# Two decoder layers on one core: the order around the second norms, and the place of a branch hint

## The chip, the core and the metric

One NeuronCore of a Trainium2 chip runs the whole program in one launch. TensorE (PE in the profile, its weight loads PEld) multiplies matrices, VectorE (DVE), ScalarE (ACT) and GpSimd (POOL) work on tiles of 128 partitions in SBUF, sums of products land in PSUM banks, and SyncE (SP) issues most of the DMA transfers between HBM and SBUF. The metric is the device time of one launch in microseconds (us).

## What is computed

Two layers of a decoder, 512 tokens of width 1024 in float32. Layer 0 mixes tokens with two groups of recurrent heads, layer 1 with sparse attention over chosen keys. Behind each mixer stand a norm, a mixture of 16 experts (each token goes to two of them) and a second norm:

```
x = LN(alpha*x + mixer(x))                 # first norm, ln1g, ln1b
x = LN(alpha*x + MoE(x))                   # second norm, ln2g, ln2b

def _layer_norm(x, g, b):
    mu, var = mean(x), mean((x - mu)**2)
    return (x - mu) * rsqrt(var + eps) * g + b

def _moe(h, ...):                          # s = sigmoid(h @ router_w), 4 groups of 4 experts
    best group, its top two experts, gate = s / sum of the two s
    for e in range(16):
        he = (silu(h @ w_gate[e]) * (h @ w_up[e])) @ w_down[e]
        y = y + comb[:, e:e+1] * he
```

## The kernel before

Tokens lie in four tiles of 128 (NT), features in eight chunks of 128 (KC). Every float32 product is made of three: a weight tile `wr` arrives by DMA, ScalarE casts it to a rounded high part `wh` (L581), the difference to it is the low part `wl` (L582, on VectorE, or on GpSimd where a letter of a string says `p`), and TensorE adds high x high, low x high and high x low (L68 to L70). `LO1 = "pvvp"` holds these letters for the four groups of layer 1's mixer weights: the first is `w1a` (972, 972 and 648 columns in three loads), the second `w1b`.

The gate (`route`, from L800) ranks the tokens of each expert with the matmuls `cum`, keeps TensorE going with the `busy` ones (L817), and makes for each expert the list of its 128 token slots with the matmuls `lst` (`lists(0, 2)`, then `lists(2, 5)`). If an expert has more than 128 tokens, `rovf` is 1 and extra blocks run. Each engine loads `rovf` into a register and branches on it (L1093 and L1094); in the runs shown the blocks are jumped over, a few hundred rows of TensorE's program. `k.soon(engine, ins)` places a branch prefetch hint for that branch on the engine behind the instruction `ins`.

The experts then run in order: gather of rows `xg` by GpSimd, transposition `xt`, products `gu`, `htp`, `yo`, and scatter of the result `ys` into Y in HBM by GpSimd's indirect DMA (L1088) with addition. The last two experts are not scattered: their `yo` is split in `wh`, `wl` and added by TensorE.

The second norm reads Y back into the tiles Z (`hy<-Y`, L1126), and for each token tile TensorE sums Z and the last experts' rows in two PSUM banks `zt` (L1136, ten matmuls a tile). `BANKS` names the banks of the tiles. VectorE's order is written out in `TAIL`, a token for each step and tile: `s` statistics (L613 to L623; ScalarE takes the square root, L621), `r` root (reciprocal and one Newton step in L631 and L632, then times -1/2 in L1151), `c` centring with the gain (L1147), `f` finish (times the root, plus b; L1155), `n` root and ScalarE's norm out of PSUM (L1167, L1169), `g`, `h`, `p` gain and bias (L1172, L1173) on VectorE and GpSimd, on VectorE alone, on GpSimd alone, `d` the tile's next use, `e` finish and store by halves (L1160). In layer 0 `d` stands for the tile's transposition `x1tp` (L1203), its split `th`, `tl`, and then layer 1's first products `pq` with `w1a`; in layer 1 for the store of the output.

```
stt(Z[i][:, cs], zp_, S[i][0][:, 0:1], g[:, cs], op0=ALU.subtract, op1=ALU.mult)   # c: L1147
stt(Z[i], Z[i], S[i][1], b, op0=ALU.mult, op1=ALU.add)                             # f: L1155
```

On SyncE the loads of `w1a` stand behind those of Z (`behind(tc, w.loads[n0], k.last_load)`), and `AFTA = "r0"` puts ScalarE's casts of `w1a` behind the square root of tile 0.

Of the kernel before, what the change touches and what calls it, by code (L numbers as in the profile page):

```python
# [15 lines left out]
ALU = mybir.AluOpType  # L16
# [19 lines left out]
ROPE, LO1 = 512, "pvvp"  # L36
PAD = 2
BANKS = ("pj pj sv sv pj pj sv sv", "pj pj sv sv sm sm sm ch")
AFTA, AFTB = "r0", "x2 y2"

TAIL = ["s0 c0 r0 f0 s1 n1 s2 n2 d0 g1 s3 g2 c3 d1 r3 f3 d2 d3", "s0 n0 s1 n1 p1 h0 s2 d0 c2 d1 s3 r2 c3 f2 d2 r3 e3"]
# [585 lines left out]
def ln_root(nc, sm, mv, v, y, _=None):  # L627

    nc.vector.reciprocal(y, y)
    a = sm.tile([P, 1], F32, name="lna", tag="lna")  # L630
    nc.vector.scalar_tensor_tensor(a, y, v, y, op0=ALU.mult, op1=ALU.mult)  # L631
    nc.vector.scalar_tensor_tensor(y, a, 3.0, y, op0=ALU.subtract, op1=ALU.mult)  # L632
    return mv[:, 0:1], y


def out_proj_ln(tc, k, L, sm, hp, proj, g, b, order):
# [3 lines left out]
    nc = tc.nc  # L640
# [52 lines left out]
    def rest():  # L693
# [5 lines left out]
        stt(rs[:, 1:2], mu, -1.0, rs[:, 0:1], op0=ALU.mult, op1=ALU.mult)  # L699
# [66 lines left out]
def route(nc, k, rp, sm, hp, lg, rest, dbg=None):  # L766
# [63 lines left out]
    k.soon(mybir.EngineType.PE, k.ranked)  # L830
# [37 lines left out]
    def lists(a, b):  # L868
        for n in range(8):
            m = nc.tensor.matmul(lst[:, a:b].rearrange("p a e -> p (a e)"), E[:, n],  # L870
                             L[:, n, a:b].rearrange("p a e -> p (a e)"), start=n == 0, stop=n == 7)
        return m
# [28 lines left out]
    lists(2, 5)  # L901
# [99 lines left out]
def moe_ln(tc, k, I, L, w, xgp, xgs, tail, dbg):  # L1001
# [3 lines left out]
    with ExitStack() as es:  # L1005
# [63 lines left out]
        def down(e):  # L1069
# [18 lines left out]
            nc.gpsimd.indirect_dma_start(out=k.Y, out_offset=bass.IndirectOffsetOnAxis(ap=tgt[:, e:e + 1], axis=0),  # L1088
# [29 lines left out]
    with ExitStack() as es:  # L1118
# [3 lines left out]
        for v, n in ((g, "ln2g"), (b, "ln2b")):  # L1122
            nc.sync.dma_start(v, I[n][L:L + 1, :].partition_broadcast(P))
        Z = [k.h[:, i] for i in range(NT)]
        for i in range(NT):
            k.last_load = nc.sync.dma_start(Z[i], k.Y[i * P:(i + 1) * P, :])  # L1126
        S, ZP = {}, {}
# [21 lines left out]
        def root(i):  # L1149
            mu, r = ln_root(nc, sm, *S[i])  # L1150
            nc.vector.tensor_scalar(r, r, -0.5, None, op0=ALU.mult)  # L1151
            S[i] = mu, r

        def finish(i):
            stt(Z[i], Z[i], S[i][1], b, op0=ALU.mult, op1=ALU.add)  # L1155

# [20 lines left out]
        step = {"s": stats, "c": centre, "r": root, "f": finish, "e": halves, "n": norm, "g": gain,  # L1177
# [32 lines left out]
def dsa(tc, k, I, es, weights, xt, dbg):  # L1210
# [25 lines left out]
    def chunks(name, grp, ncol, lo=None, late=""):  # L1236
# [6 lines left out]
        behind(tc, w.loads[n0], k.last_load)  # L1243
        k.last_load = w.loads[-1]
# [460 lines left out]
```

## Time and profile before

| | |
|---|---|
| three runs, median (least to most) | 1030.81 us (1030.23 to 1031.31) |
| the profiled execution, its own time | 1034.22 us |
| its span in the trace | 1032.5 us |
| busy: PE, DVE, ACT, POOL | 936.1, 795.6, 563.4, 309.3 us |
| DMA | 174.06 MB, mean 169 GB/s |
| mean granted TensorE clock | 0.974 |

The span is what the trace covers; the execution's own time is 1.7 us longer. A share of busy time is a mean over stages: the mixer of layer 0 up to about 400 us, its gate to 422, its experts to 582, its second norm and layer 1's mixer and gate to 840, layer 1's experts to 1003, its second norm to the end.

### The profile page before, as it was taken

Reading aid. Unit: us, or ns where it says so; the run is one execution under the profiler, and the core shown is the slowest. Engines: PE = TensorE matmul, PEld = TensorE weight load, DVE = VectorE, ACT = ScalarE, POOL = GpSimd, SP = SyncE. Lnnn points to the kernel's source line nnn. Section 1 sums busy time; section 2 is a strip of 40 time slices with the busy share of each in tenths; the row PEclk is TensorE's granted clock in tenths of the full one; section 3 lists DMA queues with packets and bytes.
Section 4 is the critical chain, followed back from the end, with each engine's and each line's share of the span. In section 5 each row is a group of like instructions: output and inputs, shape, how many; then the busy total and the mean of one; then the engine's idle time right before and its main releaser. Section 6 shows DMA issues by size and latency. Waiting matters only on the chain. (4 is left out here: it accounts for less than half of the span.)

```text
span 1032.5 us, 14694 instructions
## 1 busy us (share of the span) xinstructions
PE 936.1 (91%) x4992; PEld 716.2 (69%) x4992; DVE 795.6 (77%) x1690; ACT 563.4 (55%) x911; POOL 309.3 (30%) x235
## 2 busy tenths in 40 slices
PE   7799988997998999899999987998999879999895
PEld 5577756675776878767778667674668767777673
DVE  4637689398398666899999887699964679898886
ACT  6435473334336124588988543436761338888771
POOL 2200202003011003365555323113201335666432
PEclk9899999999899999999999989998999999999998
DMA  6223102212104487899987544102302369999963
GB/s 225 95 67 93 53 8 86 53 52 72 27 1 155 151 276 250 315 362 341 310 303 248 171 127 142 42 1 102 123 21 82 123 242 384 319 322 312 322 234 134
DMA packets 72277, 174.06 MB, mean 169 GB/s; under 512 B 24472, under 2 KB 25784, under 8 KB 72192
## 3 DMA queue, kind: packets, MB, share of 16 engines
q1 hardware_dynamic: 63840, 158.02, 43.6%
q0 software_dynamic: 8352, 15.00, 5.9%
q8 instruction: 42, 0.69, 0.3%
q14 instruction: 43, 0.35, 0.1%
HBM read 162.19 MB, written 26.21 MB: 182 GB/s over the span
## 5 line engine op out<-in xcount | busy, mean ns | idle before, releaser
L581 ACT CAST wh<-wr 128x1024 fp32r<-128x1024 f32 (+2 forms) x233 | 220.5, 955 | 91.9 <-PE pj L69 44.1
L582 DVE TENSOR_TENSOR wl<-wr,wh 128x1024 fp32r<-128x1024 f32 (+1 forms) x193 | 229.7, 1211 | 44.7 <-ACT wh L581 36.1
L582 POOL TENSOR_TENSOR wl<-wr,wh 128x1024 fp32r<-128x1024 f32 (+2 forms) x40 | 103.7, 2597 | 134.0 <-issue 64.6
L69 PE MATMUL gu<-wl,xgh 128*128 128x512 f32 x256 | 103.9, 406 | 8.6 <-PEq L1094 5.3
L68 PE MATMUL gu<-wh,xgh 128*128 128x512 f32 x256 | 102.4, 400 | 3.1 <-DVE xgl L64 2.1
L70 PE MATMUL gu<-wh,xgl 128*128 128x512 f32 x256 | 102.6, 401 | 0.1
L68 PE MATMUL pj<-xh,wh 128*128 128x512 f32 x208 | 87.1, 419 | 9.6 <-ACT xh L63 6.6
L70 PE MATMUL pj<-xh,wl 128*128 128x512 f32 x208 | 86.3, 415 | 0.0
L69 PE MATMUL pj<-xl,wh 128*128 128x512 f32 x208 | 86.2, 415 | 0.0
L1088 POOL DMA_INDIRECT Y<-ys,rtgt x28 | 53.4, 1908 | 80.0 <-ACT ys L1084 18.7
L69 PEld LDWEIGHTS gu<-wl,xgh 128*128 128x128 f32 x256 | 48.9, 191 | 22.7 <-POOL wl L582 6.2
L1014 POOL DMA_INDIRECT xg<-hD,rtgt x30 | 46.6, 1552 | 41.7 <-PEq L1094 11.9
L68 PEld LDWEIGHTS gu<-wh,xgh 128*128 128x128 f32 x256 | 48.8, 191 | 13.7 <-DVE xgl L64 2.2
L70 PEld LDWEIGHTS gu<-wh,xgl 128*128 128x128 f32 x256 | 48.9, 191 | 9.8 <-DVE xgl L64 0.5
L68 PEld LDWEIGHTS pj<-xh,wh 128*128 128x128 f32 x208 | 40.1, 193 | 19.8 <-ACT xh L63 6.6
L69 PE MATMUL yo<-wl,hth 128*128 128x512 f32 x128 | 52.2, 408 | 0.1
L68 PE MATMUL yo<-wh,hth 128*128 128x512 f32 x128 | 50.6, 396 | 1.8 <-ACT hth L63 1.6
L70 PE MATMUL yo<-wh,htl 128*128 128x512 f32 x128 | 50.1, 391 | 0.0
L64 DVE TENSOR_TENSOR xgl<-xtp,xgh 128x512 fp32r<-128x512 f32 x60 | 38.4, 681 | 11.7 <-ACT xgh L63 11.7
L70 PEld LDWEIGHTS pj<-xh,wl 128*128 128x128 f32 x208 | 39.9, 192 | 10.1 <-issue 2.0
L68 PE MATMUL pq<-wh,th 128*128 128x512 f32 (+2 forms) x128 | 46.9, 366 | 0.0
L69 PEld LDWEIGHTS pj<-xl,wh 128*128 128x128 f32 x208 | 40.1, 193 | 9.8 <-issue 1.7
(433 smaller groups left out, 2246.2 us busy)
## 6 DMA issues: line engine op xcount, KB each, us to landing
wr<-in_wgu_dram SPq DMA_DIRECT2D x102, 512.0 KB
wr<-in_wdn_dram SPq DMA_DIRECT2D x50, 512.0 KB
wr<-in_w_dram SPq DMA_DIRECT2D x52, 256.0 KB
wr<-in_wo_dram SPq DMA_DIRECT2D x16, 512.0 KB
hy<-in_wgu_dram SPq DMA_DIRECT2D x15, 512.0 KB
room<-in_wgu_dram SPq DMA_DIRECT2D x11, 512.0 KB
hy<-in_wdn_dram SPq DMA_DIRECT2D x9, 512.0 KB
hD<-hy SPq DMA_DIRECT2D x8, 512.0 KB
```

The source lines that it names most:

```text
L64: nc.vector.tensor_tensor(lo, src, hi.bitcast(F32), op=ALU.subtract))
L68: nc.tensor.matmul(out, ah, bh, start=start, stop=False)
L69: nc.tensor.matmul(out, ah, bl, start=False, stop=False)
L70: return nc.tensor.matmul(out, al, bh, start=False, stop=stop)
L581: nc.scalar.copy(h[:, s], r[:, s])
L582: (lo or nc.vector).tensor_tensor(l[:, s], r[:, s], h[:, s].bitcast(F32), op=ALU.subtract)
L1014: nc.gpsimd.indirect_dma_start(out=xg, out_offset=None, in_=k.hD, in_offset=bass.IndirectOffsetOnAxis(ap=tgt[:, e:e + 1], axis=0), bounds_ ...
L1088: nc.gpsimd.indirect_dma_start(out=k.Y, out_offset=bass.IndirectOffsetOnAxis(ap=tgt[:, e:e + 1], axis=0), in_=ys, in_offset=None, bounds_c ...
```

## The change

It does these things: the three `w1a` loads stand ahead of the Z loads on SyncE, the casts no longer wait for tile 0's root, and their low parts move from GpSimd to VectorE; the Newton step uses two operands per partition as scalars (TENSOR_SCALAR) in place of SCALAR_TENSOR_TENSOR, also in one place of the first norm; the factor -1/2 is multiplied once into the gain vector g by GpSimd, behind its last scatter, and L1151 goes; tile 3 of layer 0 sums in the banks `sm` and `ch`; in layer 1 the root of tile 2 is taken earlier, and its finish becomes a multiplication on ScalarE and an add of b on GpSimd (`k`); TensorE's branch hint moves from behind the `cum` matmuls to behind `lists(2, 5)`.

```diff
-ROPE, LO1 = 512, "pvvp"
+ROPE, LO1 = 512, "vvvp"
...
-BANKS = ("pj pj sv sv pj pj sv sv", "pj pj sv sv sm sm sm ch")
-AFTA, AFTB = "r0", "x2 y2"
+BANKS = ("pj pj sv sv pj pj sm ch", "pj pj sv sv sm sm sm ch")
+AFTA, AFTB = "", "x2 y2"
-TAIL = ["s0 c0 r0 f0 s1 n1 s2 n2 d0 g1 s3 g2 c3 d1 r3 f3 d2 d3", "s0 n0 s1 n1 p1 h0 s2 d0 c2 d1 s3 r2 c3 f2 d2 r3 e3"]
+TAIL = ["s0 c0 r0 f0 s1 n1 s2 n2 d0 g1 s3 g2 c3 d1 r3 f3 d2 d3", "s0 n0 s1 n1 p1 h0 s2 d0 c2 r2 k2 d1 s3 c3 d2 r3 e3"]
...
-    nc.vector.scalar_tensor_tensor(a, y, v, y, op0=ALU.mult, op1=ALU.mult)
-    nc.vector.scalar_tensor_tensor(y, a, 3.0, y, op0=ALU.subtract, op1=ALU.mult)
+    nc.vector.tensor_scalar(a, y, v, y, op0=ALU.mult, op1=ALU.mult)
+    nc.vector.tensor_scalar(y, a, 3.0, y, op0=ALU.subtract, op1=ALU.mult)
...
-        stt(rs[:, 1:2], mu, -1.0, rs[:, 0:1], op0=ALU.mult, op1=ALU.mult)
+        nc.vector.tensor_scalar(rs[:, 1:2], mu, rs[:, 0:1], -1.0, op0=ALU.mult, op1=ALU.mult)
...
-    k.soon(mybir.EngineType.PE, k.ranked)
...
-    lists(2, 5)
+    k.soon(mybir.EngineType.PE, lists(2, 5))
...
-            nc.gpsimd.indirect_dma_start(out=k.Y, out_offset=bass.IndirectOffsetOnAxis(ap=tgt[:, e:e + 1], axis=0),
+            k.sent = nc.gpsimd.indirect_dma_start(out=k.Y, out_offset=bass.IndirectOffsetOnAxis(ap=tgt[:, e:e + 1], axis=0),
...
+        behind(tc, nc.gpsimd.tensor_scalar(g, g, -0.5, None, op0=ALU.mult), k.sent)
         Z = [k.h[:, i] for i in range(NT)]
         for i in range(NT):
             k.last_load = nc.sync.dma_start(Z[i], k.Y[i * P:(i + 1) * P, :])
+            if i == 0:
+                k.first_z = k.last_load
...
         def root(i):
-            mu, r = ln_root(nc, sm, *S[i])
-            nc.vector.tensor_scalar(r, r, -0.5, None, op0=ALU.mult)
-            S[i] = mu, r
+            S[i] = ln_root(nc, sm, *S[i])
...
+        def shift(i):
+            nc.scalar.mul(Z[i], Z[i], S[i][1])
+            nc.gpsimd.tensor_tensor(Z[i], Z[i], b, op=ALU.add)
...
-        behind(tc, w.loads[n0], k.last_load)
-        k.last_load = w.loads[-1]
+        if n0:
+            behind(tc, w.loads[n0], k.last_load)
+            k.last_load = w.loads[-1]
+        else:
+            behind(tc, k.first_z, w.loads[-1])
```

TensorE at the end of layer 0's gate. Before, the hint stands behind the last `cum`, ahead of the `busy`, `xt` and `lst` matmuls:

```order
L827 LDWEIGHTS ones_1371
L827 MATMUL cum<-rM,ones_1371 128x16
L1701 BRANCH_PREFETCH_HINT
L817 MATMUL busy<-c_ident 128x128 x7
L844 MATMUL xt_3817<-xg_3416,hy 128x128 x8
L870 LDWEIGHTS rE
```

At the branch, before:

```order
L870 LDWEIGHTS rE
L870 MATMUL lst<-rL,rE 128x48
L1093 TENSOR_LOAD rovf
L1094 COMPARE_AND_BRANCH
L929 LDWEIGHTS re
```

After, the last `lst` matmuls, the hint, the load of the register and the branch:

```order
L869 LDWEIGHTS rE
L869 MATMUL lst<-rL,rE 128x48
L869 LDWEIGHTS rE
L869 MATMUL lst<-rL,rE 128x48
L1709 BRANCH_PREFETCH_HINT
L1092 TENSOR_LOAD rovf
L1093 COMPARE_AND_BRANCH
L928 LDWEIGHTS re
```

The hint has moved past all of the lists. In layer 1 the same move leaves ten `gu` matmuls and the register load between hint and branch.

TensorE in layer 0's second norm, at the end of the sums of tile 2. Before, the transposition of tile 0 stands ahead of tile 3's ten `zt`:

```order
L1136 MATMUL zt<-wh,onehot 128x512
L1136 MATMUL zt<-wl,onehot 128x512
L1203 MATMUL x1tp<-c_ident,hy 128x128 x8
L1136 MATMUL zt<-hy,c_ident 128x512
L1136 MATMUL zt<-wh,onehot 128x512
```

(Seven more `zt` and then `pq` follow.) After, the last two `zt` of tile 3 stand ahead of the transposition:

```order
L1138 MATMUL zt<-wh,onehot 128x512
L1138 MATMUL zt<-wl,onehot 128x512
L1207 MATMUL x1tp<-c_ident,hy 128x128 x8
L68 MATMUL pq<-wh,th 128x324
L69 MATMUL pq<-wl,th 128x324
```

So 40 `zt` run in one piece, and the first products `pq` follow the transposition of tile 0 directly.

VectorE at the start of the same norm, before (`wl<-yo` are the last expert's low parts):

```order
L64 TENSOR_TENSOR wl<-yo,wh 128x512 x2
L613 BN_STATS bst<-zt 128x6 x2
L619 BN_AGGR bmv<-bst 128x2
L623 TENSOR_SCALAR lnv<-bmv 128x1
L1147 SCALAR_TENSOR_TENSOR hy<-zt,bmv,xg_3417 128x512 x2
L629 RECIPROCAL lny<-lny 128x1
L631 SCALAR_TENSOR_TENSOR lna<-lny,lnv 128x1
L632 SCALAR_TENSOR_TENSOR lny<-lna,lny 128x1
L1151 TENSOR_SCALAR lny<-lny 128x1
L1155 SCALAR_TENSOR_TENSOR hy<-hy,lny,xg_3418 128x1024
```

After, with the low parts of `w1a` (972, 972 and 648 columns):

```order
L582 TENSOR_TENSOR wl<-wr,wh 128x972
L64 TENSOR_TENSOR wl<-yo,wh 128x512 x2
L582 TENSOR_TENSOR wl<-wr,wh 128x972
L613 BN_STATS bst<-zt 128x6 x2
L582 TENSOR_TENSOR wl<-wr,wh 128x648
L619 BN_AGGR bmv<-bst 128x2
L623 TENSOR_SCALAR lnv<-bmv 128x1
L1149 SCALAR_TENSOR_TENSOR hy<-zt,bmv,xg_3417 128x512 x2
L629 RECIPROCAL lny<-lny 128x1
L631 TENSOR_SCALAR lna<-lny,lnv 128x1
L632 TENSOR_SCALAR lny<-lna,lny 128x1
L1155 SCALAR_TENSOR_TENSOR hy<-hy,lny,xg_3418 128x1024
```

Three low parts have come in, the third between the statistics and their aggregate, the two root steps have changed their kind, and the row of L1151 is gone. (Lines of after count from its own file.)

## Rows read from the trace of the kernel before

**Rows 1.** Busy time by stage: layer 0's experts, its second norm with the start of layer 1's mixer, layer 1's experts. Each row: from:to in us, length, busy us of PE, PEld, DVE, ACT, POOL with counts, granted TensorE clock, DMA share, GB/s.

```profile
422.00:582.00 160.00, 154.10 (x726) 123.34 (x727) 148.31 (x163) 132.81 (x183) 84.15 (x43) 0.99 0.86 293
582.00:640.00 58.00, 47.08 (x266) 38.97 (x265) 49.99 (x109) 24.29 (x45) 16.74 (x8) 0.93 0.50 168
840.00:1003.00 163.00, 153.33 (x709) 118.30 (x710) 142.15 (x157) 132.58 (x183) 88.75 (x43) 0.99 0.92 319
```

**Rows 2.** The chain of work that ended last, in order of time: start us, duration us, what.

```profile
842.70 11.68 DMA wr<-in_wdn_dram
...
1006.88 7.39 PE zt L1136 x24
```

**Rows 3.** The loads of `rovf` (L1093) and the branch on it (L1094) as each engine's sequencer ran them in both layers (PEldq is TensorE's, DVEq VectorE's, SPq SyncE's): ns min/median/max, start of the first (layer 0) and of the last.

```profile
L1093 PEldq TENSOR_LOAD <-rovf x2: 310/404/497, 418.4 to 833.0; - x2
...
L1094 SPq EVENT_SEMAPHORE  x18: 17/17/17, 425.2 to 839.6; - x18
L1094 PEldq COMPARE_BRANCH  x2: 393/3399/6405, 419.0 to 833.4; - x2
L1094 SPq COMPARE_BRANCH  x2: 68/69/70, 419.1 to 832.9; - x2
L1094 DVEq COMPARE_BRANCH  x2: 68/70/72, 420.5 to 833.1; - x2
L1094 DVEq EVENT_SEMAPHORE  x2: 21/21/21, 421.1 to 836.2; - x2
```

**Rows 4.** DMA queues by window: first queue 8, of kind instruction, in 409.2 to 419.1 (packets, MB, share); then the lines of 819.2 to 833.4 where queue 8 would stand, between queue 0 and queue 14; then queue 8 in 833.4 to 839.8.

```profile
q8 instruction: 1, 0.02, 0.6%
...
q0 software_dynamic: 144, 0.19, 5.2%
q14 instruction: 3, 0.02, 0.9%
...
q8 instruction: 1, 0.02, 1.1%
```

**Rows 5.** TensorE's timeline at the gates of layer 0 and layer 1: start us, duration, engine, line, operation, count, and in brackets the idle time before it with what ended it.

```profile
409.38 0.24 PE L827 MATMUL cum<-rM,ones 128*128 128x16 bf16 x4
...
421.95 0.51 PE L68 MATMUL gu<-wh,xgh 128*128 128x512 f32 x1 [2.13 <-DVE xgl L64]
...
839.98 0.76 PE L69 MATMUL gu<-wl,xgh 128*128 128x512 f32 x1 [5.35 <-PEq L1094]
```

**Rows 6.** TensorE's waits from 422 to 582: engine, line, who waited <- for whom: us in all, times, longest.

```profile
PE htp L1063 <- DVE hh L1056: 3.3, 10, 1.2
```

**Rows 7.** SyncE's timeline at the start of the second norm of layer 0: DMA issues.

```profile
578.00 1.75 SPq L1126 DMA_DIRECT2D hy<-Y  x4
579.85 1.75 SPq L574 DMA_DIRECT2D wr<-in_w1a_dram  x3
```

**Rows 8.** GpSimd's timeline in the second norm of layer 0; the lines L631 and L632 (ns min/median/max, first and last start); VectorE's timeline in that norm.

```profile
588.71 6.00 POOL L582 TENSOR_TENSOR wl<-wr,wh 128x972 fp32r<-128x972 f32 x3 [15.11 <-DMA wr<-in_w1a_dram]
...
L631 DVE SCALAR_TENSOR_TENSOR lna<-lny,lnv x16: 201/219/2035, 375.3 to 1026.9; 128x1 f32<-128x1 f32 x16
...
L632 DVE SCALAR_TENSOR_TENSOR lny<-lna,lny x16: 140/159/2189, 375.5 to 1027.2; 128x1 f32<-128x1 f32 x16
...
593.25 0.15 DVE L1151 TENSOR_SCALAR lny<-lny 128x1 f32<-128x1 f32 x1
593.44 2.35 DVE L1155 SCALAR_TENSOR_TENSOR hy<-hy,lny,xg 128x1024 f32<-128x1024 f32 x1
...
603.11 1.22 DVE L1172 TENSOR_TENSOR hy<-hy,xg 128x1024 f32<-128x1024 f32 x1
```

**Rows 9.** TensorE's and GpSimd's timelines in the same norm: the first and the last of the first thirty `zt`, the tile transposes `x1tp`, the first product `pq`; then the second add of L1173.

```profile
582.60 1.02 PE L1136 MATMUL zt<-hy,c_ident 128*128 128x512 f32 x2
...
593.12 0.40 PE L1136 MATMUL zt<-wl,onehot 128*128 128x512 f32 x1
595.85 1.09 PE L1203 MATMUL x1tp<-c_ident,hy 128*128 128x128 f32 x8 [2.33 <-DVE hy L1155]
599.57 2.07 PE L1136 MATMUL zt<-hy,c_ident 128*128 128x512 f32 x2 [2.63 <-ACT hy L1169]
...
605.39 0.31 PE L68 MATMUL pq<-wh,th 128*128 128x324 f32 x1
...
607.61 1.03 PE L1203 MATMUL x1tp<-c_ident,hy 128*128 128x128 f32 x8
...
614.09 0.60 PE L1203 MATMUL x1tp<-c_ident,hy 128*128 128x128 f32 x4
...
608.02 2.40 POOL L1173 TENSOR_TENSOR hy<-hy,xg 128x1024 f32<-128x1024 f32 x1 [1.16 <-DVE hy L1172]
```

**Rows 10.** The line L840, which makes 128x128 tables: ns min/median/max, first and last start.

```profile
L840 DVE TENSOR_SCALAR pick<-c_iota,rs x4: 268/1534/2930, 820.3 to 823.4; 128x128 f32<-128x128 f32 x4
```

**Rows 11.** The end of layer 1: GpSimd's and VectorE's timelines.

```profile
1018.27 3.01 POOL L1172 TENSOR_TENSOR hy<-hy,xg 128x1024 f32<-128x1024 f32 x1 [20.93 <-ACT hy L1169]
1021.36 2.34 POOL L1173 TENSOR_TENSOR hy<-hy,xg 128x1024 f32<-128x1024 f32 x1
...
1025.57 1.27 DVE L1155 SCALAR_TENSOR_TENSOR hy<-hy,lny,xg 128x1024 f32<-128x1024 f32 x1
...
1027.58 1.41 DVE L1160 SCALAR_TENSOR_TENSOR hy<-hy,lny,xg 128x512 f32<-128x512 f32 x2
```

More of the change, by code (lines that the diff above doesn't have):

```diff
@@ L1176, in moe_ln @@
             total(i)
-        step = {"s": stats, "c": centre, "r": root, "f": finish, "e": halves, "n": norm, "g": gain,
+        step = {"s": stats, "c": centre, "r": root, "f": finish, "e": halves, "k": shift, "n": norm, "g": gain,
                 "h": lambda i: gain(i, (nc.vector, nc.vector)), "p": lambda i: gain(i, (nc.gpsimd, nc.gpsimd)),
```

## The prediction

> **What bounds the kernel now.** I read the stage table first, because the change sits in four places with different limits [rows 1]. In layer 0's experts (422 to 582 us) TensorE is busy 154.10 of 160 us: what is late there ends the stage later. In layer 1's experts (840 to 1003) the DMA share is 0.92, and the chain that ended last [rows 2] shows why that is the row to look at: from 842.70 on it consists of weight loads, then it goes over the scatters into Y and their reload to the sums `zt` at 1006.88, and behind them to VectorE. Between them, from 582 to 640, TensorE is busy 47.08 of 58: nobody is the bound, and what counts is who waits last.
>
> The run profiled took 1034.22 us for a span of 1032.5 and lies 3.4 us above the median of 1030.81 (runs 1030.23 to 1031.31), more than those three differ. The sums below are differences, and I take them off the median.
>
> **1. The branch behind the gate (layer 0).** All engines jump over the overflow blocks. TensorE's COMPARE_BRANCH took 0.393 us in one layer and 6.405 in the other, VectorE's and SyncE's 0.07 each [rows 3]; what follows a branch tells the rest: SyncE branched at 419.1 and did its next thing at 425.2, 6.0 us later; VectorE branched at 833.1 and went on at 836.2, 3.0 later; in layer 0 it needed 0.6. So a jump costs either half a microsecond or 3.0 to 6.4. The DMA windows fit [rows 4]. Queue 8 is of the kind instruction, and I read it as TensorE's, since one packet of it moved just while TensorE's long jump waited (833.4 to 839.8). Between the hint of layer 0, which stands behind the `cum` matmuls (the last from 409.38, [rows 5]), and the branch at 419.0 it moved one packet too; in layer 1, between the hint at 819.2 and the branch at 833.4, none: that window has no q8 line. So the hint brought the page in layer 0, and in layer 1 it did nothing.
>
> The change moves the hint behind the last `lst` matmul. In layer 0 that is directly ahead of the TENSOR_LOAD at 418.4, 0.6 us ahead of the branch where it was some 10 us. If a page takes as long as the three slow jumps, 3.0, 6.0 or 6.4 us from about 418.3, TensorE goes on at 421.3, 424.3 or 424.7. Nothing is lost until 421.95, since the first `gu` waits for VectorE's `xgl` until then [rows 5]. The cost is 0, 2.4 or 2.8 us; a hint that does nothing gives 419.0 + 6.4 - 421.95 = 3.5. I take **+2.4**: SyncE's 6.0 was a jump at this very moment, with the same weight loads in flight, and two of three rows lie there. It carries through: TensorE is idle for 5.9 of the stage's 160 us, the 2.1 of the first `gu` among them, and 3.3 of the rest are ten waits of `htp` for VectorE's `hh`, which moves along [rows 6].
>
> [...]
>
> **2. The same branch in layer 1.** The hint now stands behind `lists(2, 5)` with ten `gu` matmuls between it and the load of `rovf`, 1.4 us ahead of the branch. If it works, TensorE resumes up to 1.4 earlier than 839.98 [rows 5]. SyncE's last semaphore of this line is at 839.6 in any case [rows 3], its own loads in flight, and the next 130 us hang on its weight loads. I take **0**, bounds -1.0 (TensorE frees buffers earlier) and 0.
>
> **3. Second norm of layer 0.** The three `w1a` loads were issued at 579.85, behind the Z loads at 578.00 [rows 7], which wait for Y. Now they stand ahead and need only their buffers. Their casts move ahead of the square roots on ScalarE, and their low parts from GpSimd to VectorE. Today GpSimd's lows run 588.71 to 594.71, and meanwhile VectorE's two root steps with two tensor operands took 2.04 and 2.19, the longest of their lines, against medians of 0.22 and 0.16, and `finish(0)` 2.35 where the others took 1.27 [rows 8]. That is 3.85 + 1.08 = 4.9 us of waiting for GpSimd. The edit pays one thing back: VectorE does 972 + 972 + 648 columns itself, at 1.22 us for 1024 about 3.1 us. The first falls in its idle 580 to 583, the second at 584.2 just ahead of the statistics that wait for `zt` until 586.4, the third between stats(0) and its aggregate: only that one is on the path, 0.77 us. The dropped multiplication by -1/2 (L1151) saves 0.15 + 0.04 per tile.
>
> My walk for tile 0: stats end 587.1, third low 587.9, aggregate and centre 589.6, root 590.2, finish 591.4; before, it ended at 595.79. TensorE isn't there yet: `zt(3)` now has banks of its own and runs on behind the thirty others, which end at 593.5, to 597.1 (ten more at the 3.6 us that ten took). So `x1tp(0)` starts at 597.1, later than before (595.85), but `pq(0)` at 598.4 rather than 605.39 [rows 9], and it isn't cut by the 2.63 us wait for ScalarE's `norm`. The next limit is the pair of adds on GpSimd (L1173, 2.40 each): `mult(1)` on VectorE stands behind tile 0's two `tl` splits; `x1tp(0)` ends at 598.2, and with ScalarE's `th` (some 1.4), `tl` (1.29) and itself (1.22) `mult(1)` ends about 602.1, the add 604.5, so `x1tp(1)` comes at 604.6 (607.61 before), add(2) ends 608.2 instead of 610.42, `x1tp(2)` 608.3, `x1tp(3)` 611.9 (614.09). GpSimd's two adds in a row set the pace, so the 7 us at `pq(0)` shrink to **-2.2**. Bounds: -0.9 (ScalarE or the `tl` splits make `mult(1)` 1.3 us later) and -4 (the 4.9 less 0.8, all of it kept). The new GpSimd multiplication g*(-1/2) I cost at nothing: GpSimd sat idle for the 15.11 us ahead of 588.71 [rows 8]. If it holds a weight split on VectorE, that is once one GpSimd op, 2.4 us at most.
>
> The root steps become TENSOR_SCALARs. One of that kind, L1151 at 593.25, took 0.15 us while GpSimd's third low ran, so a 128x1 TENSOR_SCALAR isn't held. [...]
>
> **4. End of layer 1.** Behind the last `zt` VectorE is alone on the path. It sheds `finish(2)` (1.27) and L1151 (0.19 for each of four tiles, three of them on the path): -1.8. But b of tile 2 is now added by GpSimd behind its work for tile 1, which ends at 1023.70 now, and behind a ScalarE multiplication: 1023.9 + 2.34 = 1026.3. `halves(3)` reads two SBUF tensors and can't run beside it. It starts at about 1026.3 instead of 1027.58 [rows 11]: **-1.2**, bounds -1.8 and -0.4 (GpSimd's 3.01 for the other op).
>
> **Sum.** +2.4 + 0 - 2.2 - 1.2 = -1.0, of a measurement that tells about 0.2% (2.1 us) from no change: 1033.2 for the run profiled, and 1030.81 - 1.0 = **1029.8 us** for the median.
>
> **Rivals.** *The late hint costs nothing* (0.33): the page comes within 3.6 us, as VectorE's did in layer 1 (3.0). Then -2.2 - 1.2 = -3.4, 1027.4 us. Against it: SyncE's 6.0 at the same time. *More than that in the norm* (0.10): the loads of `w1b`, next on SyncE, wait for a low part of `w1a` and come earlier, and everything up to the bound of -4 arrives: 2.4 - 4 - 1.2 = -2.8, 1028.0 us. Against it stand GpSimd's two adds in a row. *Slower* (0.12): the hint in front of the branch does nothing and costs the full 3.5, and `mult(1)` is held behind the `tl` splits, which leaves -0.9 in the norm, with the low bound at the end: 3.5 - 0.9 - 0.4 = +2.2, 1033.0 us. It decides from the point where TensorE's first `gu` of layer 0 starts later than 425 us. [...] My own forecast has 0.40; with that case at the same side of the bounds it makes 0.45 for no change, with a range of its own of 1028.8 to 1032.
>
> **The range.** 1026.8 to 1032.6: it takes in both faster cases and the slow end of my own, and leaves out the slower case and the far ends of two terms at once.
>
> **What would show it.** TensorE's COMPARE_BRANCH of layer 0 at 4 to 6 us and the first `gu` at 424 to 425 (step 1); the longest wait of TensorE in that stage grown from 2.1 to about 4.5. In layer 1 a branch of 4 to 5 us, and weight loads that start at 839.7 as before (step 2). Relative to the first `zt`: 40 `zt` in one run, roots of 0.2 us, no GpSimd at 588 to 594, `x1tp(3)` 2.2 earlier (step 3). `halves(3)` starting right when GpSimd's add ends (step 4). Wrong would make it a first `gu` at 422, or a `x1tp(1)` no earlier than 25 us behind the first `zt`.

## The result: slower by half a per cent

The changed kernel took 1038.81 us (median of 20 runs, 1032.48 to 1046.94), the kernel before 1033.3 (20 runs, 1030.23 to 1040.26): a ratio of 1.0056, 95% interval 1.0033 to 1.0079, 5.8 us (5.5 by the medians). The forecast was 1029.8 us, between 1026.8 and 1032.6; 2.5 of the 9.0 us between it and the measurement lie in its base, the 1030.81 us of three runs, and 6.5 in the change. The execution profiled took 1038.55 us, with a span of 1036.8 (before: 1034.22 and 1032.5), so the pair of traces differs by 4.3 us. The starts in the two timelines say where; each number is the distance in us between two events on TensorE, so that nothing ahead of a stretch shifts it. The last column is the same distance in three more kernels, which differ from the kernel before in the hint alone: they show how far a stretch moves by itself (`x1tp(i)` is the start of tile i's transposition).

| stretch | before | after | forecast | measured | without a hint, late hint alone, hint in the middle (experiments 1 and 3) |
|---|---|---|---|---|---|
| start to first `cum` of layer 0 | 409.13 | 408.29 | 0 | -0.84 | 409.88, 408.40, 409.35 |
| first `cum` to first `gu` (lists, branch) | 12.82 | 17.24 | +2.4 | +4.42 | the hint itself was moved |
| first `gu` to first `zt` (experts) | 160.65 | 162.35 | 0 | +1.70 | 167.05, 162.05, 161.94 |
| first `zt` to `x1tp(3)` (second norm) | 31.49 | 30.25 | -2.2 | -1.24 | 31.43, 29.77, 30.03 |
| `x1tp(3)` to first `cum` of layer 1 | 205.01 | 206.17 | 0 | +1.16 | 202.52, 204.71, 202.46 |
| first `cum` of layer 1 to its first `zt` | 187.78 | 187.54 | 0 | -0.24 | 185.96, 186.39, 187.26 |
| first `zt` of layer 1 to the end of the span | 25.57 | 24.94 | -1.2 | -0.63 | 25.57, 25.58, 25.58 |

So the changed kernel lies clearly outside of these four traces in three stretches: the branch, the one behind the norm and the end of layer 1. Its norm is no shorter than that of the late hint alone and of the hint in the middle, which have the norm of before. In these two GpSimd's low parts of `w1a` came 6.90 and 7.67 us behind the first `zt`, not 6.11, and tile 0's roots were through ahead of them. With the hint in the middle (experiment 3, kernel before):

```profile
591.86 6.52 POOL L582 TENSOR_TENSOR wl<-wr,wh 128x972 fp32r<-128x972 f32 x3 [15.66 <-ACT wh L581]
...
590.61 0.22 DVE L631 SCALAR_TENSOR_TENSOR lna<-lny,lnv 128x1 f32<-128x1 f32 x1
590.86 0.16 DVE L632 SCALAR_TENSOR_TENSOR lny<-lna,lny 128x1 f32<-128x1 f32 x1
...
584.19 1.10 PE L1136 MATMUL zt<-hy,c_ident 128*128 128x512 f32 x2 [1.17 <-DMA hy<-Y]
614.22 0.60 PE L1203 MATMUL x1tp<-c_ident,hy 128*128 128x128 f32 x4
```

The 4.9 us that the roots and `finish(0)` lost in the trace of before [rows 8] are thus one way that this race can end.

The branch after the change, as TensorE's sequencer ran it: ns min/median/max, first and last start (lines are those of the new file, the register load is L1092, the branch L1093). Then TensorE's timeline, and queue 8 in 417.6 to 425.4. These answer to [rows 3 to 5].

```profile
L1709 PEldq BRANCH_PREFETCH_HINT  x2: 41/46/50, 417.5 to 836.6; - x2
...
L1093 PEldq COMPARE_BRANCH  x2: 4549/5840/7131, 418.2 to 839.2; - x2
```

```profile
425.53 0.77 PE L68 MATMUL gu<-wh,xgh 128*128 128x512 f32 x1 [6.55 <-PEq L1093]
```

```profile
q8 instruction: 1, 0.02, 0.7%
```

The hint came at 417.5, 0.7 us ahead of the branch; one packet of queue 8 moved while the branch waited, 7.13 us where it had been 0.39, and the first `gu` starts at 425.53 behind the sequencer instead of 421.95 behind `xgl`. In layer 1 the hint stood 2.6 us ahead (836.6 and 839.2), the jump took 4.55 instead of 6.41, and the stretch to `zt` is 0.24 us shorter.

TensorE in the second norm of layer 0 after the change (answers to [rows 9]):

```profile
587.88 1.10 PE L1138 MATMUL zt<-hy,c_ident 128*128 128x512 f32 x2 [1.10 <-DMA hy<-Y]
...
602.26 1.03 PE L1207 MATMUL x1tp<-c_ident,hy 128*128 128x128 f32 x8
604.21 0.42 PE L68 MATMUL pq<-wh,th 128*128 128x324 f32 x1 [0.92 <-ACT hy L1173]
609.71 1.09 PE L1207 MATMUL x1tp<-c_ident,hy 128*128 128x128 f32 x8 [1.70 <-POOL hy L1177]
...
613.29 1.10 PE L1207 MATMUL x1tp<-c_ident,hy 128*128 128x128 f32 x8 [1.69 <-DVE tl L64]
...
618.13 0.60 PE L1207 MATMUL x1tp<-c_ident,hy 128*128 128x128 f32 x4
```

Against the trace of before three things are new. The first `zt` waits 1.10 us for Z; so it does, for 0.96 to 1.30 us, in five of the nine traces with the loads behind Z. `x1tp(0)` starts 14.38 us behind the first `zt` (13.25 before), right behind the 40 `zt`, though VectorE had finished tile 0 at 596.8. And TensorE is busy for 1.66 of the 3.58 us from `x1tp(1)` to `x1tp(2)`, and runs at a lower granted clock from there to `x1tp(3)`, which takes 4.84 us. Those two stretches (columns as in [rows 1]), then the second one before:

```profile
609.71:613.29 3.58, 1.66 (x10) 1.15 (x10) 3.58 (x7) 1.26 (x3) 2.36 (x1) 1.00 0.00 0
613.29:618.13 4.84, 4.84 (x24) 4.83 (x25) 4.28 (x9) 3.25 (x6) 0.00 (x0) 0.65 0.34 108
```

```profile
610.48:614.09 3.61, 3.61 (x27) 3.60 (x27) 3.61 (x12) 2.92 (x5) 0.00 (x0) 1.00 0.09 20
```

### The profile page after: what moved, and what is told of

Its sections match the earlier page's. It is cut to its first block, busy times and chain, and to the rows that moved or that the text cites. A ratio compares the mean times of both kernels' runs of the same rounds, so it can differ in the third digit from the quotient of the medians.

```text
span 1036.8 us, 14686 instructions
## 1 busy us (share of the span) xinstructions
PE 938.9 (91%) x4992; PEld 720.8 (70%) x4992; DVE 794.2 (77%) x1684; ACT 563.3 (54%) x912; POOL 310.3 (30%) x235
## 5 line engine op out<-in xcount | busy, mean ns | idle before, releaser
L582 DVE TENSOR_TENSOR wl<-wr,wh 128x1024 fp32r<-128x1024 f32 (+2 forms) x196 | 233.9, 1213 | 49.2 <-ACT wh L581 41.6
L582 POOL TENSOR_TENSOR wl<-wr,wh 128x1024 fp32r<-128x1024 f32 x37 | 96.7, 2619 | 115.9 <-issue 59.0
L70 PE MATMUL pq<-wh,tl 128*128 128x512 f32 (+2 forms) x128 | 47.8, 374 | 0.0
```

Of the source, the lines that this page charges most:

```text
L70: return nc.tensor.matmul(out, al, bh, start=False, stop=stop)
L582: (lo or nc.vector).tensor_tensor(l[:, s], r[:, s], h[:, s].bitcast(F32), op=ALU.subtract)
```

## The experiments

Each kernel was timed beside the kernel before on the same chip. The runs of one kernel spread over 9 to 16 us, so that a ratio is known to 0.2 to 0.3%. The distances in the traces are steadier, but each is one trace, and the table above shows by how much they move in the experts and the norm; a difference in a trace is called an effect only where it comes back in a second pair or has its wait beside it.

**1. The hint alone, and no hint.** The kernel before with

```diff
-    k.soon(mybir.EngineType.PE, k.ranked)
-    lists(2, 5)
+    k.soon(mybir.EngineType.PE, lists(2, 5))
```

> The kernel before, with TensorE's branch hint alone moved behind lists(2, 5). Theory A (the late hint is the loss): from the first cum of layer 0 to the first gu it takes 17.2 us as in the changed kernel, 4.4 more than before (12.8), with a COMPARE_BRANCH of about 7 us; the median is 4 to 5 us above before. Theory B (the loss comes from the reordered second norm): the gate of layer 0 shows the same long jump, but most of it is made up before 582 us, and the median is within 2 us of before.

and with the first of these lines taken out and nothing put in:

> The kernel before without any hint on TensorE. If a hint half a microsecond ahead is as good as none: a jump of 6.4 us in layer 0 as in layer 1, gu 3.5 to 4.4 us later than before, the same time as with the late hint alone. If the late hint does harm of its own (it fetches something that the jump then has to wait for): 1 to 1.5 us faster than with the late hint. Layer 1's jump 6.4 us as before, since the early hint did nothing there.

Measured: 1036.61 us against 1032.52, ratio 1.0040 (1.0010 to 1.0070), with the late hint; 1039.66, ratio 1.0067 (1.0037 to 1.0098), with none. The late hint's branch and first `gu`, then those of the kernel without a hint:

```profile
L1700 PEldq BRANCH_PREFETCH_HINT  x2: 41/46/50, 417.6 to 834.1; - x2
L1093 PEldq COMPARE_BRANCH  x2: 6330/6812/7294, 418.3 to 836.7; - x2
...
425.88 0.77 PE L68 MATMUL gu<-wh,xgh 128*128 128x512 f32 x1 [6.78 <-PEq L1093]
```

```profile
L1093 PEldq COMPARE_BRANCH  x2: 6408/6770/7132, 419.7 to 841.7; - x2
...
426.36 0.77 PE L68 MATMUL gu<-wh,xgh 128*128 128x512 f32 x1 [5.78 <-PEq L1093]
```

From `cum` to `gu` it is 17.48 us with the late hint and 16.48 without one (12.82 before), so the hint's move alone brings the whole loss of this stretch: theory A holds for it. Whether the late hint does harm of its own is not shown. Behind it the jump of layer 0 took 6.85 to 7.29 us in three kernels; without a hint it took 6.41 in layer 0 and 7.13 in layer 1 of the same trace. So 0.7 us ahead a hint is worth about as much as none. That the kernel without a hint came out 3 us above the one with the late hint is not its branch: its trace has the experts at 167.05 us, 5 longer than here. Why is open; the two intervals overlap, and one kernel of experiment 7 has the experts at 166.45 in its trace.

**2. The hint back in the changed kernel**, twice.

```diff
+    k.soon(mybir.EngineType.PE, k.ranked)
-    k.soon(mybir.EngineType.PE, lists(2, 5))
+    lists(2, 5)
```

> The changed kernel with TensorE's hint put back behind the cum matmuls. Theory A: 4.4 us are won back, the layer-0 jump is 0.4 us, the median is 1 to 2 us below before (norm 1.2, end 0.6) if the wait for Z does not show, about equal to before if it does. Theory B: it stays 3 to 5 us above before.

> The changed kernel with only the hint back, run again beside the others, since its first profile had a low clock ahead of the change. By theory D: x1tp(0) at 14.4 and x1tp(3) at 30 to 31 us behind the first zt, median 0 to 2 us above before. If its first median (0.37% above before) was an accident of the clock: equal to before or below.

Measured: 1036.59, ratio 1.0037 (1.0011 to 1.0063), and 1036.34, ratio 1.0061 (1.0035 to 1.0087). `cum` to `gu` is back at 12.81 and 12.83, yet the kernel stays 4 to 5 us above before. Theory A isn't enough: there is a second loss in the rest of the change. The norm takes 31.95 and 31.97 us to `x1tp(3)`, more than before.

**3. A hint between the two.** In the changed kernel and in the kernel before, the hint behind `lists(0, 2)`:

```diff
     m = lists(0, 2)
+    k.soon(mybir.EngineType.PE, m)
```

> The changed kernel with TensorE's hint behind lists(0, 2), some 5 us ahead of layer 0's branch and 7 ahead of layer 1's. Theory A' (a hinted page is ready 7 to 8 us after the hint, whatever stands between: 417.5 to 425.4 in the changed kernel): layer 0 jump 2 to 3 us long, over at about 13.0 after the first cum, gu at 13 to 13.5 (17.2 in the changed kernel, 12.8 before); layer 1 jump under 1 us, but the experts there no earlier, since SyncE waits for its own loads. Median 3 to 4.5 us below the changed kernel. Theory C (only a hint 10 us ahead is served): gu at 16.5 or later.

> The kernel before with the hint behind lists(0, 2). Theory A': the same jumps as in the changed kernel with this hint; layer 0 at most 0.5 us later than before, layer 1's gu 3 to 5 us earlier counted from its first cum, of which at most 1 us is left at the first zt of layer 1. Median within 1 us of before. If layer 1's long jump does count, 3 us below before.

Measured: 1035.13, ratio 1.0043 (1.0018 to 1.0068), and 1031.68, ratio 1.0016 (0.9988 to 1.0045). The hint and the branch, in the changed kernel and in the kernel before:

```profile
L1710 PEldq BRANCH_PREFETCH_HINT  x2: 41/46/50, 412.1 to 828.5; - x2
L1094 PEldq COMPARE_BRANCH  x2: 2417/4644/6872, 417.1 to 835.5; - x2
```

```profile
L1701 PEldq BRANCH_PREFETCH_HINT  x2: 41/46/50, 414.2 to 824.0; - x2
L1094 PEldq COMPARE_BRANCH  x2: 2017/4654/7292, 419.3 to 831.1; - x2
```

In layer 0 the jump is over at 419.5 and 421.3, 7.4 and 7.1 us after the hint, and `gu` comes at 12.88 and 12.90 behind `cum`, where it waits 2.1 us for `xgl`: theory A' holds there in the traces, and 5 us are lead enough. The median is 3.7 below the changed kernel's, as forecast, but the ratio to before only falls from 1.0056 to 1.0043. In layer 1 the expectation failed: with 7 us of lead the jump took 6.87 and 7.29. Over the kernels layer 1's jump lasted between 2.7 and 7.6 us whatever its hint, and the time to `zt` there stayed between 185.6 and 189.8.

**4. The w1a group alone**, and without moving the loads. The kernel before with `LO1 = "vvvp"`, `AFTA = ""` and the new `behind` lines; then the same without the `behind` lines, so that the loads stay behind Z.

```diff
-ROPE, LO1 = 512, "pvvp"
+ROPE, LO1 = 512, "vvvp"
-AFTA, AFTB = "r0", "x2 y2"
+AFTA, AFTB = "", "x2 y2"
```

> The kernel before with only the w1a group of edits: loads ahead of Z, casts ahead of the roots, low parts on VectorE. Theory A: no loss; the GpSimd stretch at 588 to 594 is gone, finish(0) 4 us earlier, x1tp(3) up to 1 us earlier counted from the first zt, the median 0 to 2 us below before. Theory B: the early loads share the DMA engines with the last scatters, Z is issued 1 to 3 us later counted from the first gu, zt waits about 1 us for it, and the median is 1 to 3 us above before.

> The kernel before with the low parts of w1a on VectorE and the casts ahead of the roots, but the loads behind Z as before. If the early w1a loads are what makes the last scatters and Z late: Z issued at 156 us behind the first gu as before (158 to 159 with the loads first), no wait of zt for Z, first zt at 160.7; VectorE then waits for the loads at 587 to 589 and the norm gains less than 2.4. If the scatters are late for another reason: Z at 158 to 159 again.

Measured: 1032.95, ratio 1.0016 (0.9986 to 1.0047), and 1036.12, ratio 1.0036 (1.0010 to 1.0062). With the loads first, `x1tp(3)` comes 29.04 us behind the first `zt`, 2.45 earlier than in the trace of before and 0.7 earlier than in the best of the four traces with the old norm; `zt` itself starts 1.0 later, and 0.9 is lost again behind the norm. Scatters, loads and the wait for Z, loads first:

```profile
562.60 1.65 POOL L1088 DMA_INDIRECT Y<-ys,rtgt  x1 [4.67 <-DMA Y<-ys,rtgt]
572.52 1.56 POOL L1088 DMA_INDIRECT Y<-ys,rtgt  x1 [5.16 <-DVE wl L582]
...
559.05 1.72 SPq L574 DMA_DIRECT2D wr<-in_w1a_dram  x3
578.69 1.75 SPq L1126 DMA_DIRECT2D hy<-Y  x4
...
PE zt L1138 <- DMA hy<-Y: 1.9, 1, 1.9
```

and the loads behind Z:

```profile
565.01 1.64 POOL L1088 DMA_INDIRECT Y<-ys,rtgt  x1 [4.67 <-DMA Y<-ys,rtgt]
571.95 1.56 POOL L1088 DMA_INDIRECT Y<-ys,rtgt  x1 [2.17 <-ACT wh L581]
...
578.05 1.75 SPq L1126 DMA_DIRECT2D hy<-Y  x4
```

The next-to-last scatter waits for the one before it; for the last one the profile names other engines (VectorE, ScalarE), and that it waits in the same way is read from the distances. The last two stand 9.9 us apart with 1.3 MB of loads just ahead, 6.9 with the loads behind Z, and 7.0 in the kernel before. The eight traces of this study with the loads first, the changed kernel's among them, have 7.4 to 10.2; the nine with the loads behind Z have 6.8 to 7.6, but for the one without a hint (9.5). So by these distances the early loads hold up the scatter. How much of it reaches Z is less clear. In this pair Z is issued 158.2 and 156.2 us behind the first `gu` (156.05 before). But seven of the nine traces with the loads behind Z have it at 157.7 to 160.3, since there the next-to-last scatter itself was later, and the eight with the loads first at 158.2 to 159.4. The first `zt` then waits 0.96 to 2.70 us for Z with the loads first, and 0 to 1.30 with the loads behind Z. In the five traces where it waited 1.86 us or more, the granted clock in the 3.6 us behind was 0.53 to 0.59 and `x1tp(0)` came 1.4 to 1.7 later than with the same order at full clock. With the loads behind Z the norm took 33.07 us: VectorE's lows of `w1a` then follow loads issued at 579.90 instead of 559.05, and TensorE's `zt` waited 2.8 us for VectorE's centring (L1147), a wait that the traces with the loads first and of before don't have.

**5. Without the new banks and the new roots.** The changed kernel with the hint back and

```diff
-BANKS = ("pj pj sv sv pj pj sm ch", "pj pj sv sv sm sm sm ch")
+BANKS = ("pj pj sv sv pj pj sv sv", "pj pj sv sv sm sm sm ch")
```

and the two root steps as SCALAR_TENSOR_TENSOR; then with the banks alone put back.

> The changed kernel with the hint back behind cum, tile 3's sums in the banks of before and the roots as SCALAR_TENSOR_TENSOR again; the w1a group, g times -1/2 and the end of layer 1 stay. If the banks and the scalar operands bring nothing (mult(1) stood at 18.0 and 18.1 us behind the first zt without and with them): the norm of layer 0 as with the w1a group alone, x1tp(3) at 29 us behind the first zt, roots 0.22 and 0.16 us, median equal to the changed kernel with the hint back or up to 1 us below. If they bring something: x1tp(3) 1 us later than that kernel's and the median above it.

> The changed kernel with the hint back behind cum and tile 3's sums in the banks of before; everything else of the change stays. Theory D (tile 3's ten zt ahead of x1tp(0) cost the norm 3 us: x1tp(0) stood at 10.8 behind the first zt without them and at 14.4 to 16.1 with them, x1tp(3) at 27.2 and 30.3 to 32.0): x1tp(3) at 27 to 28, the end of layer 1 at 25.0 behind its first zt as in the changed kernel, median 1.5 to 3.5 us below before and 3 to 4 below the same kernel with the new banks. If the gain at x1tp(3) came from the roots' form or from the clock: x1tp(3) at 30.

Measured: 1031.36, ratio 0.9994 (0.9971 to 1.0016), and 1031.01, ratio 1.0007 (0.9981 to 1.0033). On the same chip as the second, the kernel with the new banks (experiment 2, its repeat) had 1036.34: the old banks are worth 5 us of median there. Hint and banks put back, the loss is gone, but the gain of 1.5 to 3.5 us that was expected did not come. `x1tp(0)` and `x1tp(3)` with the old banks, and then with the new ones:

```profile
582.89 2.00 PE L1139 MATMUL zt<-hy,c_ident 128*128 128x512 f32 x2 [2.54 <-DMA hy<-Y]
...
595.32 1.03 PE L1208 MATMUL x1tp<-c_ident,hy 128*128 128x128 f32 x8
...
611.67 0.60 PE L1208 MATMUL x1tp<-c_ident,hy 128*128 128x128 f32 x4
```

```profile
582.11 1.93 PE L1139 MATMUL zt<-hy,c_ident 128*128 128x512 f32 x2 [2.43 <-DMA hy<-Y]
...
598.16 1.04 PE L1208 MATMUL x1tp<-c_ident,hy 128*128 128x128 f32 x8
...
609.20 1.69 PE L1208 MATMUL x1tp<-c_ident,hy 128*128 128x128 f32 x8 [1.70 <-DVE tl L64]
614.08 0.60 PE L1208 MATMUL x1tp<-c_ident,hy 128*128 128x128 f32 x4
```

Counted from the first `zt`: `x1tp(0)` 12.43 against 16.05, `x1tp(1)` 21.61 against 23.50, `x1tp(3)` 28.78 against 31.97. Theory D holds in the traces: with banks of its own, tile 3's ten `zt` (3.6 us) go ahead of `x1tp(0)`, and what hangs on it (`th`, `tl`, `mult(1)`, GpSimd's add) moves back, by 1.9 us. The rest of the 3.2 us is the clock: from `x1tp(2)` to `x1tp(3)` it was granted at 1.00 with the old banks and at 0.65 with the new ones, 3.60 against 4.88 us. All four traces of kernels with the new banks and the `w1a` group show this 0.65, and no other trace does. The first kernel, with the old form of the roots too, has `x1tp(3)` at 27.20; its expectation let it stand at 29 or later.

The roots show at the end of layer 1. GpSimd and VectorE there, with SCALAR_TENSOR_TENSOR:

```profile
1016.74 2.34 POOL L1178 TENSOR_TENSOR hy<-hy,xg 128x1024 f32<-128x1024 f32 x1
...
1017.48 1.62 DVE L631 SCALAR_TENSOR_TENSOR lna<-lny,lnv 128x1 f32<-128x1 f32 x1
```

and in the changed kernel:

```profile
1026.24 2.34 POOL L1177 TENSOR_TENSOR hy<-hy,xg 128x1024 f32<-128x1024 f32 x1
1028.77 2.34 POOL L1159 TENSOR_TENSOR hy<-hy,xg 128x1024 f32<-128x1024 f32 x1 [0.18 <-ACT hy L1158]
...
1026.98 0.27 DVE L631 TENSOR_SCALAR lna<-lny,lnv 128x1 f32<-128x1 f32 x1
...
1031.12 1.42 DVE L1164 SCALAR_TENSOR_TENSOR hy<-hy,lny,xg 128x512 f32<-128x512 f32 x2
```

Under the same GpSimd add the old form ends with it (1019.10 and 1019.08), the new one takes 0.27. From the first `zt` to the end it is 26.12 us with the old roots and 24.94 in the changed kernel. The last row is step 4 of the prediction: `halves(3)` starts at 1031.12, when GpSimd's add for tile 2 ends (1031.11). But VectorE's own last root step, 0.21 us from 1030.87, ends at 1031.08, and the 0.04 us between are those of before (1027.54 and 1027.58), so that a wait for the add is not shown.

**6. The roots alone.** The kernel before with

```diff
-    nc.vector.scalar_tensor_tensor(a, y, v, y, op0=ALU.mult, op1=ALU.mult)
-    nc.vector.scalar_tensor_tensor(y, a, 3.0, y, op0=ALU.subtract, op1=ALU.mult)
+    nc.vector.tensor_scalar(a, y, v, y, op0=ALU.mult, op1=ALU.mult)
+    nc.vector.tensor_scalar(y, a, 3.0, y, op0=ALU.subtract, op1=ALU.mult)
```

> The kernel before with the two root steps as TENSOR_SCALAR, nothing else. If a 128x1 TENSOR_SCALAR is not held by GpSimd: L631 and L632 of tile 0 take 0.27 and 0.21 while GpSimd's lows of w1a run (2.04 and 2.19 before), finish(0) is held instead until GpSimd is through its op, x1tp(0) up to 2 us earlier and x1tp(3) 0 to 1 us earlier, median 0 to 1 us below before. If it is held: 2 us each again and no change.

Measured: 1030.51 against 1031.66, ratio 0.9992 (0.9969 to 1.0016); `x1tp(3)` 28.65 us behind the first `zt`, 2.84 earlier than in the trace of before. VectorE and GpSimd at tile 0, and tile 1's root steps:

```profile
587.50 0.27 DVE L631 TENSOR_SCALAR lna<-lny,lnv 128x1 f32<-128x1 f32 x1
587.81 0.22 DVE L632 TENSOR_SCALAR lny<-lna,lny 128x1 f32<-128x1 f32 x1
588.06 0.15 DVE L1151 TENSOR_SCALAR lny<-lny 128x1 f32<-128x1 f32 x1
588.25 3.12 DVE L1155 SCALAR_TENSOR_TENSOR hy<-hy,lny,xg 128x1024 f32<-128x1024 f32 x1
...
593.38 0.27 DVE L631 TENSOR_SCALAR lna<-lny,lnv 128x1 f32<-128x1 f32 x1
593.69 0.21 DVE L632 TENSOR_SCALAR lny<-lna,lny 128x1 f32<-128x1 f32 x1
...
588.02 6.98 POOL L582 TENSOR_TENSOR wl<-wr,wh 128x972 fp32r<-128x972 f32 x3 [15.08 <-DVE lny L632]
```

Tile 0's roots went ahead of GpSimd's first low here, so they were not put to the test, and only `finish(0)` is held, 3.12 us. The like trace with the old form is that of the late hint alone (experiment 1): roots of tile 0 ahead of the lows, `finish(0)` 3.20, `x1tp(0)` at 10.79 against 10.78 here. There a root step of tile 1 took 1.40 us under the lows, where it takes 0.21 here, and `x1tp(3)` is at 29.77. So of the 2.84 us the new form is shown to bring 1.1; the rest is how the race between roots and lows went. Where the lows come as early as before (6.02 us behind the first `zt`, in the repeat of experiment 7), the new form keeps tile 0's steps at 0.27 and 0.21 under them. These two lines of the change bring the norm to about where the `w1a` group has it, without touching a load.

**7. What is left without the losses.** The changed kernel without the w1a group, with the old banks and the hint back, twice.

> The changed kernel without the w1a group, with the old banks and the hint back: roots with scalar operands, g times -1/2, the end of layer 1. Z is issued earlier than with the w1a loads first (156 to 158.6 behind the first gu against 158 to 159.4), the norm of layer 0 gains 0 to 1 us (finish(0) still meets GpSimd's lows), the end of layer 1 0.6. Median 0.5 to 1.5 us below before; if the w1a group is worth its price, 1 to 2 us above the kernel that keeps it.

> Roots with scalar operands, g times -1/2 and the end of layer 1, without the w1a group, the banks and the late hint, again: 2 to 3 us below before, the interval of the ratio below 1.

Measured: 1028.74 against 1031.66, ratio 0.9970 (0.9948 to 0.9991), and 1029.79 against 1030.75, ratio 0.9988 (0.9963 to 1.0013). It is ahead of both kernels in the medians, and in one of two comparisons clear of no change, so that the repeat's expectation failed; its size is between 0.1 and 0.3%. `x1tp(3)` stands at 28.20 and 27.30, 3 to 4 us ahead of before where 0 to 1 was expected, and the end of layer 1 at 24.96 and 24.87.

**8. The banks alone, and the late hint with the old banks.**

> The kernel before with tile 3's new banks alone. In the kernel before finish(0) is late, so x1tp(0) stands at 13.3 us behind the first zt anyway, and 40 zt take 14.4. If the banks cost by putting ten zt ahead of x1tp(0) (theory D): x1tp(0) at 14.4 or later, 1 us later than before, pq(0) about 6 us earlier, x1tp(3) 0 to 1 us later than before's 31.5, median 0 to 2 us above before: a small loss, the 3 us come only where finish(0) is early. If pq(0) earlier is a gain by itself: x1tp(3) 1 to 2 us earlier and the median below before.

> The changed kernel with the banks of before alone put back (late hint and all else stay). If hint and banks are the two losses: gu of layer 0 at 17.2 behind the first cum, x1tp(3) at 27 to 29 behind the first zt, median 2.5 to 3.5 below the changed kernel, 2 to 3.5 above before.

Measured: 1032.74 against 1030.75, ratio 1.0013 (0.9986 to 1.0040), and 1035.91, ratio 1.0070 (1.0040 to 1.0100). With the banks alone `x1tp(0)` is at 14.36 (13.25 before), `pq(0)` at 18.07 (22.79) and `x1tp(3)` at 30.22, 1.27 earlier than before: which theory D did not expect. But in this trace `finish(0)` ends 8.3 us behind the first `zt`, as in the trace of the hint in the middle, whose `x1tp(3)` with the old banks is at 30.03, and not 13.2 as in the trace of before. Against that like trace the banks alone bring 0.2 us of loss and no gain. In the changed kernel with the old banks `x1tp(0)` is at 10.79 (14.38) and `x1tp(3)` at 27.13 (30.25), again 3.1 earlier, `gu` at 16.97 behind `cum`. Its median is only 2.9 below the changed kernel's, and no nearer to before by ratio; its trace has the stretch ahead of `cum`, which no edit of these touches, at 417.24 us with a granted clock of 0.95 there. Each loss is shown in two pairs of traces, and the medians come back to before only with both edits undone (experiment 5); how the 5.8 us are shared between the two is not told by the medians.

## Why the prediction was wrong

Two terms of the sum failed, the branch by 2.0 us and the norm by 1.0; another 2.9 us came in stretches that were put at nothing, and 0.6 at the end. Less what the start and layer 1 gave back (1.1), that is the 5.3 us between the forecast of -1.0 and the 4.3 of the two traces.

**The branch of layer 0** (step 1): right in kind, mis-sized. The forecast let what the hint brings (its page, read from one packet of queue 8 [rows 4]) take what a jump takes, 6.0 us of SyncE's, and put the first `gu` 2.4 us later. It measured 4.42, and 4.66 with the hint alone: TensorE was 7.13 us in the branch, 7.8 from the hint on, where 6.0 from the hint had been taken. The bound of 3.5 for a hint that does nothing was close to the kernel without one (16.48 against 12.82, so 3.66) and too low for the late hint. SyncE's 6.0 was a poor measure: it is the distance to SyncE's next event, and SyncE had a hint of its own 8.2 us ahead of its branch at 419.1, in the kernel before:

```profile
L1701 SPq BRANCH_PREFETCH_HINT  x2: 45/48/51, 410.9 to 821.1; - x2
```

A further 0.43 us went behind the branch: in the 20 us from the first `gu` the granted clock was 0.89 against 0.91, and all 16 `htp` lie 0.42 to 0.46 us later, counted from that `gu`. This can be more: in all four traces with a late hint or none the clock there was 0.88 to 0.90, while in seven of the other thirteen it was 1.00 and the first `htp` came 1.0 us earlier than before. The place of the hint decided the jump of layer 0: 0.39 us with the hint 9.8 us ahead of the branch, 2.02 and 2.42 with 5 us, 7.13 with 0.7, 6.41 without one.

**Layer 1's branch** (step 2): right that nothing would show, -0.24 us at the first `zt`. The shorter jump, 4.55 instead of 6.41, is not the hint's for sure: with the hint in the same place it took 6.33 (experiment 1) and 7.23 (experiment 8).

**The experts** were put at nothing and took 1.70 us more: the 0.46 us above, and 1.24 from the last `htp` to the first `zt`, where TensorE waits for Z. The prediction costed the early loads at nothing up to Z, and behind them the last scatter is later: 7.83 us behind the one before it, 6.95 in the trace of before. But five of the eight other traces with the loads behind Z have 1.1 to 1.5 us more than before there too, so that the wait is not shown to be the loads' doing.

**The second norm of layer 0** (step 3): the walk was right up to its last leg. Behind the first `zt` it had `x1tp(0)` at 14.5 us, `x1tp(1)` at 22.0, `x1tp(2)` at 25.7 and `x1tp(3)` at 29.3; they came at 14.38, 21.83, 25.41 and 30.25. What it put at the 3.6 us of before, the leg from `x1tp(2)` to `x1tp(3)`, took 4.84, at a granted clock of 0.65. It is the banks, together with the `w1a` group, that bring this about (with the banks alone that leg took 3.61 at 1.00): the 40 `zt` and `pq(0)` are done early, and TensorE then stands idle in front of `x1tp(1)` and `x1tp(2)`, 1.70 and 1.69 us, before it gets the work. That such waits alone lower the clock is not shown: with the banks alone they are 1.14 and 1.70 us, ahead of the leg at 1.00. Beside that, the walk took the new banks as they were and never asked what the norm would be without them: `mult(1)` hangs on `x1tp(0)` and starts 18.06 us behind the first `zt`, with the old banks (experiment 8) at 16.20, and `x1tp(3)` comes at 27.13. So the banks cost the norm 3.1 us, 1.9 by the order and 1.2 by the clock. The -1.24 is no gain of the change for sure, since the old norm took 29.77 to 31.49 us in four traces; the prediction read one of them as the rule.

**The roots**: the prediction held, from the 0.15 us of L1151, that a 128x1 TENSOR_SCALAR isn't held by GpSimd. The traces agree: 0.27 us under a GpSimd add, where the old form took 1.62, and 0.27 and 0.21 under the lows of `w1a` (experiment 6). It holds for these steps and not for every TENSOR_SCALAR: one of 128x4 (L604) took 0.17 us in the trace of before and 2.29 in that of after, from 634.09 on, under a low of GpSimd's that ran from 633.96 to 636.35; and L840, of 128x128, took up to 2.93 in layer 1 [rows 10], where GpSimd was at work from 820.40 to 823.14, and 0.28 in layer 0. The 0.45 for no change had 0.05 in it for adds on GpSimd that hold the new roots (1032.0 us); the traces show no such hold. The prediction took the roots for a matter of form, since the `w1a` group was to clear GpSimd away anyway; alone they bring at least 1.1 us in the norm.

**The end of layer 1** (step 4): right in the time, while the wait that it named is not shown. `halves(3)` starts with the end of GpSimd's add, 1.42 us earlier from the first `zt` (forecast 1.2), but right behind VectorE's own root too (experiment 5). That GpSimd holds an operation of this kind shows at `finish(0)`: 2.35 us in the trace of before [rows 8], 3.12 in experiment 6, both under a low of GpSimd's, and 1.28 in the changed kernel, with GpSimd idle. From `halves(3)` on, it is 5.66 us to the end of the span instead of 4.87, which the sum had as unchanged; 0.63 are left, within the bounds. Why the last part is longer is open.

**The rivals**: the slower one named the right place (a first `gu` later than 425 us decides; it was 425.53) and the price 3.5, with the norm at -0.9 (measured -1.24). It had 0.12, and its 1033.0 us were still too low. What no rival had is the wait for Z, the lower clock at the end of the norm, and the 1.2 us lost between `x1tp(3)` and the gate of layer 1, whose cause stays open.

## What to carry to other kernels

What the prefetch hint was worth in layer 0 went by how far ahead of the branch it stood: 5 or 0.7 us ahead, the jump was over 7 to 8 us behind it; 5 us were enough, since a wait of 2.1 us covered the rest, and 0.7 us ahead it was worth no more than none. In layer 1 this did not hold (6.41 us in the jump with 14 us of lead), so look at the jump itself. When two edits make the same tile earlier, and a third puts work in front of that tile's next step, price the third by itself: the banks cost 3.1 us of the norm here, 1.2 of them in a leg at a granted clock of 0.65. Read a stretch in more than one trace before pricing a wait in it: what GpSimd held up in one trace here (roots of 2.04 and 2.19 us) it let pass in another with the same norm (0.22 and 0.16). And don't take a load that is moved ahead for free while the path waits for another transfer: with the `w1a` loads first the last scatter came 7.4 to 10.2 us behind the one before it, with the loads behind Z 6.8 to 7.6 in eight of nine traces. Ask which transfer was alone there.

## What was not expected of the hardware

The time of one kernel goes with TensorE's mean granted clock. The changed kernel's 20 runs lie between 1032.48 us at 0.980 and 1046.94 at 0.957, and over all kernels a run takes some 6.3 us more for each 0.01 less (4.1 to 9.2 within single kernels). At equal clock, by one such line through 334 runs, the changed kernel is 3.4 us above before (give or take 1.0), the late hint alone 3.7, the hint back 1.5 to 1.6, that with the old banks too -0.9, the roots alone -1.9, the version of experiment 7 -2.7 and -2.2 (each give or take up to 1.4). So some 2 of the 5.8 us came with a lower clock in the changed kernel's runs. Part of that may be the change's own: behind TensorE's waits of 1.7 us in the norm the clock was 0.65 (1.00 in that leg before), behind the 6.55 us at the branch 0.89 over 20 us (0.91 before). How much can't be told from these runs, since low clocks also show in stretches that no edit touches.

Over the kernels layer 1's branch took 2.7 to 7.6 us, and behind the late hint 4.55, 6.33 and 7.23 in three of them, so its length differs from trace to trace with the hint in one place. Why it took 6.41 us there with a hint 14 us ahead (the kernel before, where queue 8 moved no packet until TensorE stood at the branch [rows 4]) and 6.87 and 7.29 with one 7 us ahead (experiment 3), while 5 us are enough in layer 0, stays open.
